# A hybrid decoder step on one core: the order of the q, k and v projections in the attention's input stage

## The chip, the core and the metric

The kernel runs on one core of a Trainium2 chip. Its time is the device time of one launch in microseconds (us), the median of several runs. The core has a matrix engine (TensorE; PE for its products, PEld for its weight loads), a vector engine (VectorE, DVE), a scalar engine (ScalarE, ACT), a third engine for elementwise work (GpSimd, POOL), and SyncE (SP), whose instruction stream issues most of the DMAs. Every engine works through its own list of instructions in order, and an instruction that waits holds back what is behind it on the same engine. The engines' working memory is SBUF, the products' results land in eight banks of PSUM, and inputs, outputs and scratch arrays lie in HBM.

## What is computed

One layer of a decoder. The input, 1024 prompt rows and 64 sample rows (1088 in all), is normalised and multiplied with one wide weight matrix `w_in`, whose columns belong to three groups of heads: a recurrent mixer (RWKV-7, here "wkv"), a short convolution, and a stick-breaking attention of 8 heads of 64. Their outputs go through an output projection, an MLP and a gated embedding.

```python
h = rmsnorm(x, g_mix)
proj = h @ w_in                                   # [wkv 1024 | convolution 768 | attention 3 x 512]
o_rw, wkv_new, shift_new = rwkv7_mixer(p_rw, ...)
cb, cc, cx = split(p_cv, 3); o_cv = short_conv_mixer(cb, cc, cx, ...)
q, k, v = [t.reshape(B, T, 8, 64) for t in split(p_sb, 3)]
q, k = rmsnorm(q, q_gain), rmsnorm(k, k_gain)     # over the 64 of each head; v is left as it is
o_sb = stick_breaking(q, k_all, v_all, past_len, sb_bias)
x = x + concat(o_rw, o_cv, o_sb) @ w_out
x = x + square(relu(rmsnorm(x, g_mlp) @ w_up)) @ w_down
x = x + sigmoid(rmsnorm(x, g_ple) @ w_ple_gate) * (p @ w_ple_proj)
```

The new k and v rows of all tokens are outputs too.

## The kernel before

All large products are made in three passes: an operand is kept as a high part (rounded to the fast 32-bit format `F32R`) and a low part (the rest), and hi*hi, lo*hi and hi*lo are added up in one bank.

The stages follow one another in the text: the input's norm and transposes; the wkv projections (`rw_tile`, lines 316 to 339, called in the loop of line 374); the wkv chunks (`wkv_prompt_chunks`, line 658, called in line 761); the attention's input stage (lines 767 to 865); then the wkv sample chunk, the convolution and the attention's first half (lines 1030 to 1032); the output projection and the rest. A scheduler makes each engine's list ahead of time by simulating the program: an instruction that stands earlier in the text goes first when it is ready in that simulation, and later ones fill the time between. So the products of the attention's input stage fill PE while the wkv work of the stage before is still going on, at places that the simulation chose and that no longer move when the program runs.

Of the wkv work two parts matter here. `wkv_base` (line 267), called in line 424, inverts small triangular blocks for all 16 chunks. It loads `base_Z` from scratch (SP, line 276), then alternates 31 times between a product (DVE, line 281, from 1 up to 961 elements per partition) and a sum (DVE, line 283), each waiting for the one before, copies the result (line 284) and stores it in `t_s` (SP, line 285). `wkv_local` (line 463) then loads a pair of chunks: `ar` and `bk` (SP, lines 483 and 486) and the inverse `TT` (line 491). Its first products are in line 508. The pool of these tiles (`kp`, line 760) is laid over the pool of `wkv_base`, which is released in line 759, so that the loads wait for the tiles that were there before.

The attention's input stage makes q (n = 0), k (n = 1) and v (n = 2) of two halves of the heads (hf = 0, 1, four heads or 256 columns each): six projections. Each has five steps (i0 = 0, 2, 4, 6, 8), of two tiles of 128 tokens, or one tile in the last step, which holds the sample rows.

- `W.load` (line 147) brings the 1024x256 weights in two pieces of 512 KB (SP, line 156), rounds them (ACT, line 158) and makes the low part (POOL, line 159). There are two buffers for each of raw piece, high and low part.
- `project` (line 782): per tile 24 products of 256 columns (PE, lines 791 to 793) into one of two banks in turn (`gemm_sb`), then a copy to a tile `nat` (ACT, line 798; five buffers). For q and k alone follow the square (ACT, line 801), the sum over each head (DVE, line 803), the root (ACT, line 804), the reciprocal (DVE, line 805) and the scaling of `nat` (DVE, line 806).
- `keep` (line 809): for k the gain is multiplied on POOL into `kg` (line 816). k and v rows go to the outputs (SP, lines 820 to 824). For v, except in the last step, each of the two tiles is split into a tile `spl`: high part on ACT (line 830), low part on DVE (line 831), a store to `v_s` on SP (line 832).
- `stack` (line 834), for q and k only and not for the last step: four transposes of `nat` on PE (line 840) into bank 2, the high part with the gain (ACT, line 842), the low part (DVE, line 843), and four stores to `stk_s`, two on ACT's and two on SP's list (line 846). `spl` and these two tiles share four buffers (tag `st`).

A stack isn't made right after its step: steps wait in a list `waiting`, and the oldest is taken out when two wait; `tc.issue_after(last.ins)` puts its transposes behind the last product of the current step in PE's list. When v comes, the list is emptied. The tiles of this stage are in a pool `sbp`, released in line 865; the convolution's pool `cv` (line 966) takes its place. The convolution uses the same two banks (line 967), the wkv sample chunk uses bank 2 (line 1030), and the attention's `prep` (line 878) loads heads 0 to 7 one after the other from `stk_s` and `v_s`.

Of the kernel before, what the change touches and what calls it, by code (L numbers as in the profile page):

```python
# [48 lines left out]
def hybrid_step(ctx: ExitStack, tc: tile.TileContext, I, O):  # L49
# [6 lines left out]
    def f(t):  # L56
        return t.bitcast(F32)
# [115 lines left out]
    w_in = I["w_in"][0]  # L173
    W = Weights(wpool)
# [139 lines left out]
    last = rp.tile([9, 1024], F32, name="last")  # L314
# [452 lines left out]
    SB0 = 1792  # L767
# [14 lines left out]
    def project(hf, n, w, i0):  # L782

        ni = min(2, 9 - i0)
        ps = gemm_sb()[:, :256 * ni]
        for i in range(ni):
            t0 = min(128 * (i0 + i), T - 128)
            o = ps[:, 256 * i:256 * i + 256]
            for k in range(8):
                a, b = (x[k // 4][:, k % 4, t0:t0 + 128] for x in hT)  # L790
                PE.matmul(o, a, w[0][:, k, :], start=(k == 0), stop=False)  # L791
                PE.matmul(o, a, w[1][:, k, :], start=False, stop=False)  # L792
                last = PE.matmul(o, b, w[0][:, k, :], start=False, stop=(k == 7))  # L793
        nat = sbp.tile([128, 2, 256], F32, name="nat", bufs=5)
        flat = nat.rearrange("p i c -> p (i c)")[:, :256 * ni]
        n4 = flat.rearrange("p (g d) -> p g d", d=64)
        m = 4 * ni
        S.copy(flat, ps)
        if n < 2:
            sq = sbp.tile([128, 512], F32, name="sq", bufs=1)  # L800
            S.square(sq[:, :256 * ni], ps)
            ss = sbp.tile([128, 8], F32, name="ss", bufs=3)
            V.reduce_sum(ss[:, :m], sq[:, :256 * ni].rearrange("p (g d) -> p g d", d=64), axis=AX.X)
            S.activation(ss[:, :m], ss[:, :m], AF.Sqrt, bias=eps_rms, scale=1.0 / 64)
            V.reciprocal(ss[:, :m], ss[:, :m])
            V.tensor_mul(n4, n4, ss[:, :m, None].to_broadcast([128, m, 64]))
        return nat, last

    def keep(hf, n, i0, nat):

        hs, cs = slice(4 * hf, 4 * hf + 4), slice(256 * hf, 256 * hf + 256)
        ni = min(2, 9 - i0)
        out = nat
        if n == 1 or n == 0 and i0 == 8:
            out = sbp.tile([128, 2, 256], F32, name="kg", bufs=2)
            G.tensor_mul(*(t.rearrange("p i c -> p (i c)")[:, :256 * ni].rearrange("p (g d) -> p g d", d=64)
                           for t in (out, nat)), gains[:, n, None, :].to_broadcast([128, 4 * ni, 64]))
        dst_p, dst_s = outs[n]
        if i0 == 8:
            SP.dma_start(new_s[n][:, cs], out[64:128, 0])  # L820
            if n:
                SP.dma_start(dst_s[0].rearrange("b j h d -> (b j) (h d)")[:, cs], out[64:128, 0])
        elif n:
            SP.dma_start(dst_p[0, 0].rearrange("t h d -> t (h d)")[i0 * 128:i0 * 128 + 256, cs]
                         .rearrange("(i p) c -> p i c", p=128), out)
        if n == 2 and i0 < 8:
            for i in range(2):
                src = nat[:, i].rearrange("p (h d) -> p h d", h=4)
                spl = sbp.tile([128, 4, 128], F32R, name="spl", tag="st", bufs=4)
                S.copy(spl[:, :, 0:64], src)  # L830
                V.tensor_sub(spl[:, :, 64:128], src, f(spl[:, :, 0:64]))
                SP.dma_start(v_s[hs, i0 + i].rearrange("h p e -> p h e"), f(spl))
# [16 lines left out]


    waiting = []
    for hf in range(2):
        for n in range(3):
            w = W.load(w_in[:, SB0 + 512 * n + 256 * hf:SB0 + 512 * n + 256 * hf + 256])
            for i0 in range(0, 9, 2):
                nat, last = project(hf, n, w, i0)
                keep(hf, n, i0, nat)
                while waiting and (len(waiting) > 1 or n == 2):
                    with tc.issue_after(last.ins):
                        stack(*waiting.pop(0))  # L860
                    if n < 2:
                        break
                if n < 2 and i0 < 8:
                    waiting.append((hf, n, i0, nat))
    sbp.release()


# [684 lines left out]
    for sl in range(4):  # L1552
        w = load(wg_[:, sl * 256:sl * 256 + 256], 8, 256)
# [35 lines left out]
```

## Time and profile before

| what | us |
|---|---|
| median of 3 runs (lowest and highest) | 1735.58 (1730.76 to 1736.79) |
| the profiled execution, its own time | 1743.91 |
| its span, first to last instruction | 1742.0 |
| PE busy in the span | 1663.5 (95%) |
| DVE busy | 1109.6 (64%) |
| ACT busy | 774.8 (44%) |
| POOL busy | 693.0 (40%) |
| mean granted TensorE clock | 0.978 of full speed |

The profile is of one execution. An engine is called busy while one of its instructions runs; the ends of PE's products are modelled and products overlap, so that PE's busy share alone doesn't tell how close it is to its peak: the distance from one product's start to the next does. "Idle before, releaser" is the time that an engine stood still and the instruction or DMA that ended the wait. Times within the span count from its first instruction. The attention's input stage runs from about 155 to 448 us.

### The profile page before, as it was taken

The numbers are of one execution on the slowest core, as the hardware profiler recorded it, in microseconds if no ns is written. First come the engines' busy times: TensorE is split into PE (matmuls) and PEld (weight loads), VectorE is DVE, ScalarE is ACT, GpSimd is POOL, SyncE is SP. The second block draws the span as 40 slices with busy tenths as digits, with TensorE's granted clock in tenths as the row PEclk, the third lists the DMA queues.
The fourth block names the chain that finished last, engine by engine and source line by source line (L and its number), as shares of the span: only waits on it lengthen the run. The fifth ranks groups of instructions, "written<-read, shape, count | busy, mean of one in ns | idle before, by whom it ended". The sixth has DMA issues, their size and how long they took to land.

```text
span 1742.0 us, 30723 instructions
## 1 busy us (share of the span) xinstructions
PE 1663.5 (95%) x11901; PEld 1496.9 (86%) x11901; DVE 1109.6 (64%) x1830; ACT 774.8 (44%) x1537; POOL 693.0 (40%) x746
## 2 busy tenths in 40 slices
PE   6999889999999889999999999998999999998998
PEld 5898888888998667888887767988899999998898
DVE  6266863554576659878754444467888878876432
ACT  6634323323353658566543433464444343443421
POOL 4133121212331654433434652376665555544210
PEclk9999999999999899999999999999999999998999
DMA  5134456434623753443244553421322232321211
GB/s 185 50 115 133 104 156 163 118 88 133 160 75 81 247 174 103 126 125 105 88 142 145 180 175 114 162 67 61 106 89 89 86 94 86 94 94 55 64 52 40
DMA packets 207059, 197.01 MB, mean 113 GB/s; under 512 B 58113, under 2 KB 172449, under 8 KB 206786
## 3 DMA queue, kind: packets, MB, share of 16 engines
q1 hardware_dynamic: 197186, 174.08, 33.5%
q0 software_dynamic: 5120, 16.78, 3.2%
q10 hardware_dynamic: 4608, 4.20, 1.0%
q8 instruction: 93, 1.52, 0.4%
q14 instruction: 52, 0.43, 0.1%
HBM read 158.02 MB, written 36.98 MB: 112 GB/s over the span
## 4 chain that ended last, share of the span: by engine, by line
PE 73%; DVE 12%; DMA 5%; issue 3%; ACT 2%; SPq 2%; POOL 1%; ACTq 0%; DVEq 0%; POOLq 0%
PE b L1087 13%; PE b L1089 13%; PE b L1088 13%; PE b L1416 3%; PE b L1415 3%; PE b L1414 3%; PE b L169 2%; PE b L170 2%; PE b L171 2%; DVE base_Q L281 2%; PE b L791 2%; PE b L792 2%; PE b L793 2%; PE b L936 1%; DMA wr<-in_w_out 1%
## 5 line engine op out<-in xcount | busy, mean ns | idle before, releaser
L1068 POOL TENSOR_TENSOR wl<-wr,wh 128x512 fp32r<-128x512 f32 x172 | 236.0, 1381 | 269.1 <-ACT wh L1067 260.2
L1067 ACT CAST wh<-wr 128x512 fp32r<-128x512 f32 x292 | 179.1, 621 | 305.2 <-PE b L1088 205.9
L1087 PE MATMUL b<-ah,wh 128*128 128x288 f32 (+1 forms) x768 | 258.9, 337 | 10.9 <-DVE x L1452 7.9
L1452 DVE TENSOR_TENSOR x<-b,x 128x288 f32<-128x288 f32 (+1 forms) x384 | 199.0, 528 | 98.4 <-PE b L1089 94.0
L1089 PE MATMUL b<-ah,wl 128*128 128x288 f32 (+1 forms) x768 | 254.8, 332 | 0.0
L1088 PE MATMUL b<-al,wh 128*128 128x288 f32 (+1 forms) x768 | 254.1, 331 | 0.0
L1087 PEld LDWEIGHTS b<-ah,wh 128*128 128x128 f32 x768 | 146.7, 191 | 25.7 <-DVE x L1452 12.5
L1087 PE MATMUL b<-nh,wh 128*128 128x512 f32 (+1 forms) x448 | 165.2, 370 | 0.1
L1088 PE MATMUL b<-nl,wh 128*128 128x512 f32 (+1 forms) x448 | 164.9, 368 | 0.3 <-DVE nl L1297 0.3
L1089 PE MATMUL b<-nh,wl 128*128 128x512 f32 (+1 forms) x448 | 164.2, 367 | 0.0
L1089 PEld LDWEIGHTS b<-ah,wl 128*128 128x128 f32 x768 | 146.7, 191 | 11.3 <-issue 0.8
L1088 PEld LDWEIGHTS b<-al,wh 128*128 128x128 f32 x768 | 147.0, 191 | 9.7 <-issue 0.8
L791 PE MATMUL b<-wh,h_hi 128*128 128x256 f32 x432 | 129.2, 299 | 0.0
L159 POOL TENSOR_TENSOR wl<-wr,wh 128x1024 fp32r<-128x1024 f32 x26 | 69.2, 2673 | 149.0 <-ACT wh L158 114.7
L792 PE MATMUL b<-wl,h_hi 128*128 128x256 f32 x432 | 127.0, 294 | 0.0
L793 PE MATMUL b<-wh,h_lo 128*128 128x256 f32 x432 | 125.9, 291 | 0.0
L169 PE MATMUL b<-h_hi,wh 128*128 128x384 f32 (+1 forms) x336 | 115.5, 344 | 1.9 <-ACT xs L330 1.2
L170 PE MATMUL b<-h_lo,wh 128*128 128x384 f32 (+1 forms) x336 | 113.2, 337 | 0.0
L171 PE MATMUL b<-h_hi,wl 128*128 128x384 f32 (+1 forms) x336 | 111.9, 333 | 0.0
L916 DVE TENSOR_TENSOR_SCAN keep<-keep,onesq 128x128 f32<-128x128 f32 (+3 forms) x64 | 94.7, 1481 | 20.9 <-POOL keep L914 19.7
L1068 DVE TENSOR_TENSOR wl<-wr,wh 128x512 fp32r<-128x512 f32 x120 | 100.6, 841 | 6.0 <-ACT wh L1067 3.1
L1068 POOL TENSOR_TENSOR wsl<-s,wsh 128x512 fp32r<-128x512 f32 x64 | 88.5, 1405 | 29.3 <-ACT wsh L1067 29.2
(417 smaller groups left out, 4326.3 us busy)
## 6 DMA issues: line engine op xcount, KB each, us to landing
wr<-in_w_up SPq DMA_DIRECT2D x64, 512.0 KB
wr<-in_w_down SPq DMA_DIRECT2D x64, 512.0 KB
wr<-in_w_in SPq DMA_DIRECT2D x26, 512.0 KB
wr<-in_w_out SPq DMA_DIRECT2D x16, 512.0 KB
xt<-in_x_prompt SPq DMA_DIRECT2D x8, 512.0 KB
stk_s<-sth ACTq DMA_DIRECT2D x32, 128.0 KB
stk_s<-stl SPq DMA_DIRECT2D x32, 128.0 KB
v_s<-spl SPq DMA_DIRECT2D x16, 256.0 KB
```

The source lines that it names most:

```text
L169: PE.matmul(ps[:, :n], wh[:, k, c], a, start=(k == 0), stop=False)
L170: PE.matmul(ps[:, :n], wh[:, k, c], b, start=False, stop=False)
L171: PE.matmul(ps[:, :n], wl[:, k, c], a, start=False, stop=(k == nk - 1))
L791: PE.matmul(o, a, w[0][:, k, :], start=(k == 0), stop=False)
L792: PE.matmul(o, a, w[1][:, k, :], start=False, stop=False)
L793: last = PE.matmul(o, b, w[0][:, k, :], start=False, stop=(k == 7))
L1067: S.copy(h3, src)
L1068: (sub or G).tensor_sub(l3, src, f(h3))
L1087: PE.matmul(ps[:, :n], w(0, k, m), a, start=(k == 0), stop=False)
L1088: PE.matmul(ps[:, :n], w(0, k, m), b, start=False, stop=False)
L1089: PE.matmul(ps[:, :n], w(1, k, m), a, start=False, stop=(k == nk - 1))
L1452: V.tensor_add(p.x[:, m, t0:t0 + n], ps[:, :n], p.x[:, m, t0:t0 + n])
```

## The change

The six projections come in another order. Before, each half of the heads has q, k, v: (hf, n) = (0,0), (0,1), (0,2), (1,0), (1,1), (1,2). After, v of both halves is first, then q and k of the first half, then q and k of the second: (n, hf) = (2,0), (2,1), (0,0), (1,0), (0,1), (1,1). The list of waiting stacks is treated alike in all steps (the oldest is taken when two wait), and what is left is stacked behind the last product of all. No instruction is added or taken away.

```diff
     waiting = []
-    for hf in range(2):
-        for n in range(3):
-            w = W.load(w_in[:, SB0 + 512 * n + 256 * hf:SB0 + 512 * n + 256 * hf + 256])
-            for i0 in range(0, 9, 2):
-                nat, last = project(hf, n, w, i0)
-                keep(hf, n, i0, nat)
-                while waiting and (len(waiting) > 1 or n == 2):
-                    with tc.issue_after(last.ins):
-                        stack(*waiting.pop(0))
-                    if n < 2:
-                        break
-                if n < 2 and i0 < 8:
-                    waiting.append((hf, n, i0, nat))
+    for n, hf in ((2, 0), (2, 1), (0, 0), (1, 0), (0, 1), (1, 1)):
+        w = W.load(w_in[:, SB0 + 512 * n + 256 * hf:SB0 + 512 * n + 256 * hf + 256])
+        for i0 in range(0, 9, 2):
+            nat, last = project(hf, n, w, i0)
+            keep(hf, n, i0, nat)
+            if len(waiting) > 1:
+                with tc.issue_after(last.ins):
+                    stack(*waiting.pop(0))
+            if n < 2 and i0 < 8:
+                waiting.append((hf, n, i0, nat))
+    for args in waiting:
+        with tc.issue_after(last.ins):
+            stack(*args)
     sbp.release()
```

## The prediction

> **What bounds the kernel now.** I read the chain that ended last, then busy time by stretches, PE's waits, and DVE's groups where the chain lies on DVE.
>
> ```profile
> PE 73%; DVE 12%; DMA 5%; issue 3%; ACT 2%; SPq 2%; POOL 1%; ACTq 0%; DVEq 0%; POOLq 0%
> ```
>
> PE carries the chain, DVE the next largest part. The stretches (PE, PEld, DVE, ACT and POOL busy with their counts, clock, DMA share, GB/s) say where PE isn't full:
>
> ```profile
> 155.00:256.00 101.00, 85.02 (x706) 83.04 (x705) 79.89 (x122) 28.96 (x55) 28.47 (x15) 0.93 0.53 143
> 256.00:290.00 34.00, 32.53 (x320) 29.56 (x318) 9.89 (x23) 7.16 (x16) 2.92 (x2) 0.90 0.68 175
> 290.00:448.00 158.00, 158.00 (x1916) 139.19 (x1916) 83.81 (x186) 53.43 (x120) 35.60 (x40) 1.00 0.44 114
> 448.00:557.00 109.00, 108.43 (x819) 98.31 (x818) 74.22 (x151) 50.03 (x110) 33.67 (x80) 0.98 0.40 107
> ```
>
> From 290 to 557 us PE is full at full clock: there only less PE work would help, and the change takes none away. From 155 to 256 us PE idles 16 of 101 us at a mean clock of 0.93. All waits of PE from 155 to 448 us (total, times, longest):
>
> ```profile
> PE b L840 <- DVE stl L843: 9.4, 3, 4.8
> PE b L442 <- DVE LT L262: 3.3, 1, 3.3
> PE b L840 <- DVE nat L806: 3.1, 1, 3.1
> PE b L621 <- ACT UV L564: 1.3, 1, 1.3
> ```
>
> So 9.4 + 3.1 = 12.5 us are the stacks' transposes, which wait for DVE. DVE is late since it runs the wkv base inversion then. Its first and last instruction, with DVE's groups between them:
>
> ```profile
> 177.62 0.16 DVE L281 TENSOR_TENSOR base_Q<-base_Z,base_X 128x1 f32<-128x1 f32 x1 [6.21 <-DMA base_Z<-l_s]
> 238.66 2.03 DVE L284 COPY base_X<-base_X 128x1024 f32<-128x1024 f32 x1
> ```
> ```profile
> L281 DVE TENSOR_TENSOR base_Q<-base_Z,base_X 128x1 f32<-128x1 f32 (+30 forms) x31 | 26.9, 867 | 6.8 <-DMA base_Z<-l_s 6.2
> L283 DVE TENSOR_REDUCE base_X<-base_Q 128x1 f32<-128x1 f32 (+30 forms) x31 | 15.5, 500 | 0.5
> L806 DVE TENSOR_TENSOR nat<-nat,ss 128x512 f32<-128x512 f32 (+1 forms) x10 | 11.4, 1140 | 0.0
> L803 DVE TENSOR_REDUCE ss<-sq 128x8 f32<-128x512 f32 (+1 forms) x10 | 6.2, 624 | 0.0
> L843 DVE SCALAR_TENSOR_TENSOR stl<-b,gainT,sth 128x512 fp32r<-128x512 f32 x6 | 4.5, 745 | 0.0
> L284 DVE COPY base_X<-base_X 128x1024 f32<-128x1024 f32 x1 | 2.0, 2028 | 0.0
> L805 DVE RECIPROCAL ss<-ss 128x8 f32<-128x8 f32 (+1 forms) x10 | 1.9, 188 | 0.0
> ```
>
> The inversion alone is 26.9 + 15.5 + 2.0 = 44.4 us and lasts 63.1 us (177.6 to 240.7), since 11.4 + 6.2 + 4.5 + 1.9 = 24.0 us of q's and k's work sit between its steps (sums overlap a little). The way from its end to the first wkv product goes through SP's list:
>
> ```profile
> 240.72 0.34 SPq L285 DMA_DIRECT2D t_s<-base_X  x1
> 242.79 1.24 SPq L846 DMA_DIRECT2D stk_s<-stl  x2
> 247.15 2.05 SPq L483 DMA_DIRECT2D ar<-ar_s  x2
> 251.85 0.98 SPq L486 DMA_DIRECT2D bk<-bk_s  x2
> ```
> ```profile
> 256.35 0.71 PE L508 MATMUL b<-ar,bk 64*128 64x128 f32 x8
> ```
>
> The loads are issued to 252.8 us; the product starts at 256.35 with no wait before it. PE had lost so much to the transposes that it got there about when the data did: the two losses are one loss seen twice, and that decides how much the change can give.
>
> **What the change does, and what each part costs.**
>
> 1. *Transposes out of the inversion's time.* With v first, nothing that PE does for two projections waits for DVE: a bank is freed by ACT's copy alone. The 12.5 us of waits go from their place. With them goes the slow clock behind each:
>
> ```profile
> 183.70 0.65 PE L840 MATMUL b<-ident,nat 128*128 128x128 f32 x4 [3.11 <-DVE nat L806]
> 186.21 0.41 PE L792 MATMUL b<-wl,h_hi 128*128 128x256 f32 x1
> 186.42 0.41 PE L793 MATMUL b<-wh,h_lo 128*128 128x256 f32 x1
> 188.31 0.28 PE L792 MATMUL b<-wl,h_hi 128*128 128x256 f32 x1
> 188.43 0.28 PE L793 MATMUL b<-wh,h_lo 128*128 128x256 f32 x1
> ```
>
> After the wait of 3.11 us starts are 0.21 us apart, and two us later 0.12. I estimate 1.6 us lost behind a wait (some 3.6 us of products at this pace), 4.8 us for the three long ones. PE would reach its place at 256.35 us up to 12.5 + 4.8 = 17.3 us sooner. That is the most that this part gives; the least is nothing, if PE then waits as long for the wkv data.
>
> [...]
>
> 2. *The inversion gets DVE sooner.* v's work on DVE is one subtraction per tile:
>
> ```profile
> L831 DVE TENSOR_TENSOR spl<-nat,spl 128x256 fp32r<-128x256 f32 x16 | 7.0, 468 | 12.6 <-ACT spl L830 12.6
> ```
>
> All 16 take 7.0 us. PE needs 48 x 0.12 = 5.8 us for a full step and 432 x 0.12 = 52 us for both of v's projections, so by about 155 + 52 + 3.3 (the wait for LT, which stays) + 2 for wkv's own products, 212 us, v is projected, and two steps of q come before the inversion ends; without their stacks that is 2 x (0.62 + 0.19 + 0.68 by the normal length of L806, an estimate from 11.4 us less the two long ones) = 3 us. The inversion would end at 177.6 + 44.4 + 7.0 + 3.0 = 232 us, 8.7 us sooner. From both sides: if none of q's steps and none of POOL's interference falls in it, 12 us sooner; if each subtraction in DVE's list waits for ACT as the 12.6 us in its row did, 4 us sooner or nothing. POOL's interference:
>
> ```profile
> 198.02 2.85 DVE L806 TENSOR_TENSOR nat<-nat,ss 128x512 f32<-128x512 f32 x1
> 201.13 2.85 DVE L281 TENSOR_TENSOR base_Q<-base_Z,base_X 128x441 f32<-128x441 f32 x1
> 204.66 1.06 DVE L281 TENSOR_TENSOR base_Q<-base_Z,base_X 128x484 f32<-128x484 f32 x1
> ```
> ```profile
> 197.92 5.22 POOL L159 TENSOR_TENSOR wl<-wr,wh 128x1024 fp32r<-128x1024 f32 x2 [34.15 <-PE b L840]
> ```
>
> While POOL makes weights' low parts, a product of 441 elements takes 2.85 us, where a larger one right after takes 1.06. The next weights are made in the inversion's time in either order, so I leave this in the 44.4.
>
> [...]
>
> 3. *What PE waits for instead.* The first wkv product can't come before the inversion's end and the 15.6 us behind it (240.7 to 256.35; stores of v take the place of the stacks' there): 232 + 15.6 = 247.6 us, or 244 with the 12 us. PE is there at 256.35 - 17.3 = 239 us, if the simulation puts as many projection products ahead of it as now. So PE waits 5 to 9 us (I take 7) once, and pays the clock once, 1.6 us. Behind that product in PE's list stand q's next steps, which are held back with it.
>
> 4. *The tail.* The stage now ends with k and its last stack, no longer with v.
>
> ```profile
> 447.20 0.28 PE L793 MATMUL b<-wh,h_lo 128*128 128x256 f32 x1
> 447.32 0.34 PE L169 MATMUL b<-h_hi,wh 128*128 128x384 f32 x1
> ```
> ```profile
> 451.73 0.48 ACT L981 COPY cc<-b 128x384 f32<-128x384 f32 x1 [1.94 <-PE b L171]
> ```
>
> The convolution follows without a gap, and its first copy, into memory that this pool leaves, waits only for its product. k's chain after the product is copy and square on ACT, 1.5 us on DVE (as above), and the gain on POOL:
>
> ```profile
> L816 POOL TENSOR_TENSOR kg<-nat,gains 128x512 f32<-128x512 f32 (+1 forms) x12 | 14.9, 1240 | 66.1 <-DVE nat L806 29.8 <-issue 12.5 <-ACT Yg L646 12.2
> ```
>
> With 1.2 us for that and an estimated 1.3 for ACT it is some 4 us, about what the convolution's first group takes (447.3 to 451.7), and two banks cover a second group: I take 1 us, between 0 and the 4 us of that chain. SP's stores for it stand ahead of the sample chunk's loads; PE being full from 448 to 557 us hides that.
>
> 5. *v's queues, which move into the inversion's time.*
>
> ```profile
> v_s<-spl SPq DMA_DIRECT2D x16, 256.0 KB
> ```
> ```profile
> ACT spl L830 <- DMA v_s<-spl: 3.6, 3, 2.8
> ```
>
> A step of v stores two such tiles and 256 KB of output, some 130 GB/s, where the first stretch shows a DMA share of 0.53: hidden. SP's stores wait for the subtraction, at most one product of the inversion late (1 to 2.9 us), and the next weights' loads stand behind them; these have a projection's 26 us. ACT's rounding waits for a buffer, and the copies that free PE's banks stand behind it. Before, that cost ACT 3.6 us and PE nothing; with four buffers, two steps' time, I take nothing. Without that cover PE would wait those 3.6 us.
>
> Sum: 17.3 - 7 - 1.6 - 1 = 7.7, about 8 us. The profiled execution took 1743.9 us (span 1742.0, 1.9 outside); it would take 1735.9. It lies 8.3 above the median of the runs shown, so the forecast is 1735.6 - 8 = 1727.6 us.
>
> **The rivals.**
>
> *All of it.* The simulation finds the wkv data later relative to the projections than the chip does, or puts more projection products ahead of them; PE never waits for L508, and only the tail is paid: 17.3 less 1 = 16 us, 1719.5. For it: the list is made anew, and four full projections are left to fill with. Against: the lists now fell out so that data and PE met at 256 us only because PE was late.
>
> *Nothing.* The inversion is no earlier (its subtractions wait for ACT, POOL stretches them), PE stands still the whole 17 us at L508 instead of at the transposes: 1735.6 within 3. For it: DVE is 80 of 101 us busy; against: 24 us of DVE work become 10.
>
> *Slower: DVE becomes late in the wkv chunks.* From 256 to 447 us DVE has now ten q or k steps:
>
> ```profile
> L803 DVE TENSOR_REDUCE ss<-sq 128x8 f32<-128x512 f32 (+1 forms) x10 | 6.3, 629 | 9.6 <-ACT sq L801 9.6
> ```
>
> After, some 18 of the 20 fall there. Each of the eight more puts up to 0.68 + 0.75 = 1.4 us (L806, L843) in front of a DVE step of the wkv chain, and PE's list is fixed. If all hit it, PE waits 11 us, and with four of these waits long enough for the slow clock, 6 more: 17 - 8 = 9 us slower, 1744.6. It decides from 8 us of such waits on. Against it: with ten steps PE waited not once from 290 to 448 us, and DVE's share there is 84 of 158, 100 of 158 after.
>
> **The numbers.** Forecast (4 to 13 us faster, 1722.6 to 1731.6) 0.46; all of it 0.18; nothing 0.18; slower 0.18. A measurement tells about 0.5%, 8.7 us, from no change. Half of the forecast's chance, 0.24, and all of the first rival's is faster by more: 0.42. The other 0.22 and "nothing" are within: 0.40. Slower 0.18. The range goes from the first rival less the runs' own 3 us and a bit, 1715, to the slower case, 1745.
>
> **What would show it.** The row L840 <- L806 or L843 is gone from PE's waits before 240 us, and the inversion's copy (L284) ends near 232 us, not 240.7. PE has one new wait, before L508, of 5 to 9 us, which ends near 247. ACT no longer waits for L803 until v is done. From 290 us on PE has no waits, and the convolution's first product follows the last projection within 1 us, at about 439. I am wrong if L284 ends after 238 us, if PE's new wait is over 12 us or absent, or if waits for DVE appear among the wkv chunks.

## The result, and the profile after

The changed kernel took 1747.33 us (median of 6 runs, 1742.29 to 1748.82), the kernel before 1735.82 us beside it (6 runs, 1730.76 to 1738.13): ratio 1.0063 with a 95% interval of 1.0044 to 1.0083. It is 11.5 us slower, outside the predicted range of 1715 to 1745 us.

Most of what the prediction named as a sign came. PE's waits in the changed kernel from 150 us to its last projection (total, times, longest) are two:

```profile
PE b L508 <- DMA bk<-bk_s: 11.3, 1, 11.3
PE b L442 <- DVE LT L262: 3.5, 1, 3.5
```

The 12.5 us of L840 are gone and the one new wait stands before L508, but it is longer than the 5 to 9 us forecast. There is no wait for DVE among the wkv chunks. The timelines of the changed kernel show where the new wait comes from (start, length, engine, instruction); DVE's, SP's and PE's:

```profile
228.37 1.16 DVE L284 COPY base_X<-base_X 128x1024 f32<-128x1024 f32 x1
```
```profile
229.55 0.33 SPq L285 DMA_DIRECT2D t_s<-base_X  x1
229.98 0.46 SPq L820 DMA_DIRECT2D new<-nat  x1
230.49 1.43 SPq L822 DMA_DIRECT2D out<-nat  x1
232.02 1.16 SPq L156 DMA_DIRECT2D wr<-in_w_in  x1
233.27 1.04 SPq L483 DMA_DIRECT2D ar<-ar_s  x2
...
237.07 0.87 SPq L486 DMA_DIRECT2D bk<-bk_s  x2
```
```profile
227.57 0.28 PE L793 MATMUL b<-wh,h_lo 128*128 128x256 f32 x1
239.17 1.23 PE L508 MATMUL b<-ar,bk 64*128 64x128 f32 x8 [11.33 <-DMA bk<-bk_s]
```

The inversion ends at 229.5 us, the data are there 9.6 us later, and PE stands still from 227.8 us on. The prediction had put the data at 247.6 us, 15.6 us behind the inversion, and PE at 239 us: both came sooner, PE by more. Behind the wait the granted clock was 0.50 until 247.0 us, 7.9 us long, with products 0.21 us apart instead of 0.12; that is some 3.4 us lost (an estimate from these figures). PE comes so early because less work stands ahead of L508 in its list. The groups of PE's instructions up to that product, kernel before and changed kernel (busy, mean ns, idle before):

```profile
L791 PE MATMUL b<-wh,h_hi 128*128 128x256 f32 x200 | 59.6, 298 | 0.0
L792 PE MATMUL b<-wl,h_hi 128*128 128x256 f32 x199 | 58.3, 293 | 0.0
L793 PE MATMUL b<-wh,h_lo 128*128 128x256 f32 x199 | 58.0, 292 | 0.0
L840 PE MATMUL b<-ident,nat 128*128 128x128 f32 x32 | 5.9, 316 | 12.5 <-DVE stl L843 9.4 <-DVE nat L806 3.1
```
```profile
L791 PE MATMUL b<-wh,h_hi 128*128 128x256 f32 x179 | 52.2, 292 | 0.0
L793 PE MATMUL b<-wh,h_lo 128*128 128x256 f32 x179 | 51.2, 286 | 0.0
L792 PE MATMUL b<-wl,h_hi 128*128 128x256 f32 x179 | 51.0, 285 | 0.0
```

598 projection products and 32 transposes became 537 products and none. The new list has 61 products (7.3 us at 0.12 us from start to start) behind L508 that stood ahead of it; that the scheduler's simulation had the inversion end earlier too is the likely reason, and isn't shown. PE is at L508 28.5 us sooner (227.8 against 256.35): 12.5 us are the waits, 7.3 these products, and the other 8.7 the 32 transposes and the slow clock behind the waits, which weren't told apart.

The two profiled executions differ by only 2.7 us (1743.91 and 1746.60), since the one before lay 8 us above its median. So the comparison is made with a second pair, profiled side by side on one other chip (the runs before_third and after_third below, ratio 1.0080), cut at the last projection's last product (here at its end, in the table further down at its start), the output projection's first product (L1087), the attention's last (L946) and the first product of the gated embedding's stage (L1414). First the kernel before (us, then busy time and count of PE, PEld, DVE, ACT, POOL, the granted clock, DMA share, GB/s); its second row is the first 17 us behind the last projection:

```profile
150.00:441.30 291.30, 276.75 (x2954) 252.18 (x2953) 174.25 (x335) 89.52 (x191) 66.79 (x57) 0.97 0.51 134
441.30:458.30 17.00, 17.00 (x104) 17.00 (x103) 10.37 (x32) 4.14 (x7) 5.73 (x6) 1.00 0.73 196
458.30:585.00 126.70, 117.36 (x912) 103.52 (x911) 87.95 (x165) 69.26 (x157) 44.02 (x106) 0.95 0.44 130
585.00:890.00 305.00, 298.36 (x1520) 250.50 (x1519) 230.40 (x296) 184.03 (x357) 129.59 (x168) 0.98 0.40 121
890.00:1188.60 298.60, 289.75 (x1864) 235.49 (x1863) 142.98 (x219) 130.31 (x244) 147.94 (x138) 0.99 0.44 136
1188.60:1733.00 544.40, 523.97 (x3727) 508.26 (x3725) 375.70 (x674) 214.11 (x434) 250.63 (x199) 0.99 0.26 81
```

The changed kernel:

```profile
150.00:438.80 288.80, 271.50 (x2947) 248.72 (x2946) 172.49 (x334) 88.46 (x187) 63.24 (x56) 0.96 0.50 131
438.80:455.80 17.00, 10.09 (x59) 9.45 (x59) 14.53 (x34) 5.04 (x9) 6.71 (x4) 0.87 0.69 183
455.80:593.00 137.20, 125.81 (x964) 112.00 (x964) 87.97 (x160) 68.68 (x156) 43.78 (x107) 0.95 0.43 130
593.00:902.80 309.80, 300.31 (x1531) 251.55 (x1530) 243.45 (x303) 184.62 (x363) 139.61 (x170) 0.99 0.40 120
902.80:1201.20 298.40, 289.44 (x1853) 234.98 (x1852) 138.06 (x218) 128.23 (x241) 146.50 (x137) 0.98 0.44 136
1201.20:1746.00 544.80, 526.30 (x3727) 509.93 (x3725) 378.47 (x674) 215.08 (x434) 249.96 (x199) 0.99 0.26 81
```

That is the account of the 13.0 us between these two spans (1732.9 and 1745.9): the last projection 2.5 us sooner; from it to L1087 154.2 instead of 143.7 us, 10.5 more; the attention's second half 4.8 more; nothing behind it (-0.2 and +0.4). The front's gain is small because the idle time stayed: PE idles 17.3 us from 150 us to the last projection, 14.6 before the change. And in the first 17 us behind it PE runs 59 instructions where it ran 104. Of the 10.5 us 9.0 are idle time of PE (18.3 against 9.3 us); the rest is busy time, in which the eight transposes of the last two stacks, which now stand behind the last projection, have a part.

The three longest waits of that stretch, kernel before and then the changed one:

```profile
PE b L946 <- DVE o L950: 4.5, 2, 3.5
PE b L936 <- DVE wtl L61: 1.5, 1, 1.5
PE b L907 <- ACT keep L910: 1.1, 1, 1.1
```
```profile
PE b L907 <- DMA stk_q<-stk_s: 6.2, 1, 6.2
PE b L946 <- DVE o L950: 4.5, 3, 2.7
PE b L936 <- DVE beta L918: 3.2, 1, 3.2
```

What PE stands behind is seen in the first profile of the changed kernel: SP's timeline, then DVE's and POOL's.

```profile
442.22 0.47 SPq L873 DMA_DIRECT2D bias<-in_sb_bias  x1
447.14 1.23 SPq L846 DMA_DIRECT2D stk_s<-stl  x2
448.42 0.59 SPq L888 DMA_DIRECT2D stk_k<-stk_s  x1
...
450.26 0.79 SPq L888 DMA_DIRECT2D stk_q<-stk_s  x1
```
```profile
440.68 1.93 DVE L281 TENSOR_TENSOR base_Q<-base_Z,base_X 16x25 f32<-16x25 f32 x1
...
442.84 2.14 DVE L281 TENSOR_TENSOR base_Q<-base_Z,base_X 16x36 f32<-16x36 f32 x1
...
445.23 0.24 DVE L281 TENSOR_TENSOR base_Q<-base_Z,base_X 16x49 f32<-16x49 f32 x1
...
446.39 0.73 DVE L843 SCALAR_TENSOR_TENSOR stl<-b,gainT,sth 128x512 fp32r<-128x512 f32 x1
```
```profile
440.16 4.75 POOL L159 TENSOR_TENSOR wl<-wr,wh 128x1024 fp32r<-128x1024 f32 x2
```

SP issues nothing from 442.7 to 447.1 us: at the head of its list stands the store of a low part of k (L846), which DVE makes only at 446.39 us, though its high part was through on ACT at 441.95: DVE goes through the sample chunk's small inversion first, whose products are stretched while POOL makes the convolution's weights (16x25 elements take 1.93 us and 16x36 2.14, against 0.24 for 16x49 right behind). Behind that store stand the loads of the attention's first head, and PE stands at their first product (L907). In the kernel before, v's steps were the last, and the same inversion ran (452 to 463 us in the first profile) under products of the convolution, of which 120 stand ahead of the attention's first.

### The profile page after: what moved, and what is told of

Its sections match the earlier page's. It is cut to its first block, busy times and chain, and to the rows that moved or that the text cites. A ratio compares the mean times of both kernels' runs of the same rounds, so it can differ in the third digit from the quotient of the medians.

```text
span 1744.9 us, 30708 instructions
## 1 busy us (share of the span) xinstructions
PE 1655.5 (95%) x11901; PEld 1490.2 (85%) x11901; DVE 1114.0 (64%) x1830; ACT 773.1 (44%) x1537; POOL 701.8 (40%) x746
## 4 chain that ended last, share of the span: by engine, by line
PE 77%; DVE 10%; DMA 4%; issue 3%; ACT 2%; POOL 1%; SPq 1%; another core or an unknown queue 0%; ACTq 0%; DVEq 0%; POOLq 0%
PE b L1087 13%; PE b L1088 13%; PE b L1089 13%; PE b L1416 3%; PE b L1415 3%; PE b L1414 3%; PE b L793 3%; PE b L791 3%; PE b L792 3%; PE b L169 2%; PE b L170 2%; PE b L171 2%; PE b L936 2%; PE b L508 1%; DVE base_Q L281 1%
## 5 line engine op out<-in xcount | busy, mean ns | idle before, releaser
L1068 POOL TENSOR_TENSOR wl<-wr,wh 128x512 fp32r<-128x512 f32 x172 | 245.3, 1434 | 300.4 <-ACT wh L1067 246.3
L1087 PE MATMUL b<-ah,wh 128*128 128x288 f32 (+1 forms) x768 | 258.4, 337 | 14.9 <-DVE x L1452 12.3
L1089 PE MATMUL b<-ah,wl 128*128 128x288 f32 (+1 forms) x768 | 253.9, 331 | 0.0
L1087 PEld LDWEIGHTS b<-ah,wh 128*128 128x128 f32 x768 | 145.8, 190 | 32.2 <-DVE x L1452 18.4
L1087 PE MATMUL b<-nh,wh 128*128 128x512 f32 (+1 forms) x448 | 164.3, 368 | 2.5 <-DVE x L1375 2.5
L1089 PE MATMUL b<-nh,wl 128*128 128x512 f32 (+1 forms) x448 | 163.5, 365 | 0.0
L1089 PEld LDWEIGHTS b<-ah,wl 128*128 128x128 f32 x768 | 146.1, 190 | 11.0
```

The source lines that it names most:

```text
L1068: (sub or G).tensor_sub(l3, src, f(h3))
L1087: PE.matmul(ps[:, :n], w(0, k, m), a, start=(k == 0), stop=False)
L1089: PE.matmul(ps[:, :n], w(1, k, m), a, start=False, stop=(k == nk - 1))
```

## The experiments

The first theory, "the tail": k at the stage's end costs what the front gained. Its rival, "the lists": moving v makes every later list anew, and the loss lies there. The five groups of kernels below ran on a chip each, the kernel before beside them. This table gives for each the start of the last projection's last product, and the time from there to L1087, to the attention's last product, to L1414 and to the end (us, from the traces' first and last starts of these lines):

| run | last projection | to L1087 | to L946's last | to L1414 | to the end |
|---|---|---|---|---|---|
| before_again | 445.8 | 142.4 | 304.6 | 286.1 | 543.7 |
| tail_only | 445.5 | 152.6 | 306.0 | 285.0 | 544.9 |
| one_v_first | 435.2 | 147.9 | 311.1 | 285.2 | 549.2 |
| act_stores | 437.7 | 155.4 | 307.9 | 286.7 | 544.7 |
| att_later | 435.6 | 148.0 | 323.6 | 311.8 | 544.6 |
| b_att_later | 452.7 | 139.7 | 320.1 | 312.0 | 544.9 |
| rule_only | 443.6 | 140.9 | 303.8 | 300.1 | 547.7 |
| no_last_stacks | 434.3 | 151.6 | 308.8 | 299.4 | 547.5 |
| after_again | 435.6 | 155.9 | 309.2 | 309.2 | 544.7 |
| flush_soon | 440.7 | 151.9 | 310.5 | 306.8 | 549.4 |
| q_last | 437.1 | 153.3 | 309.1 | 310.6 | 544.8 |
| one_v_rule | 436.5 | 148.0 | 307.1 | 311.3 | 544.6 |
| before_third | 441.1 | 144.0 | 305.0 | 298.5 | 544.4 |
| after_third | 438.5 | 154.5 | 309.8 | 298.4 | 544.7 |
| base_early | 457.1 | 150.7 | 307.3 | 296.3 | 546.2 |
| b_base_early | 448.1 | 148.2 | 300.1 | 295.1 | 545.0 |
| rule_again | 444.8 | 138.4 | 303.2 | 286.5 | 542.2 |
| q_v_k | 445.1 | 142.6 | 308.9 | 284.0 | 544.6 |

### The same kernel again (before_again)

> The kernel before once more, unchanged. Its first profiled execution took 1743.9 us, 8 us above the median of its runs (1735.8), while that of the changed kernel (1746.6) lay at its median (1747.3); so a comparison of those two traces shows only 2.7 of the 11.5 us. Either theory expects a median within 3 us of 1735.8, and a profiled execution near it shows which stretch the 8 us came from. It also gives the ratio that two equal kernels show here: 1.000 within 0.0015.

1.0003 (0.9984 to 1.0022). This span is 19.4 us shorter than that of the first profile (1722.6 and 1742.0), and only 2.9 us of it lie ahead of the attention's end: the stage with the gathers behind it takes 286.1 us, not 297.1, and the rest 543.7, not 549.3. So profiles of different chips are compared here up to the attention's end, not behind it.

### k at the end, front as before (tail_only)

```diff
-    for n, hf in ((2, 0), (2, 1), (0, 0), (1, 0), (0, 1), (1, 1)):
+    for n, hf in ((0, 0), (1, 0), (2, 0), (2, 1), (0, 1), (1, 1)):
```

> The order is q, k of the first half, v of both halves, then q and k of the second half: the inversion meets q and k as in the kernel before, and the stage ends as in the changed kernel. Theory 'the tail' (k's last steps and stacks meet the sample chunk's inversion on DVE and stand in SP's list ahead of the loads of the attention's first head): the transposes still wait some 9 to 13 us for DVE before 240 us, PE again stands 4 to 8 us at the attention's first product (L907), and the kernel is 6 to 16 us slower than before, 1742 to 1752 us. Rival 'the lists' (the loss comes in later stages, whose lists are made anew, from v being early): no wait of over 2 us at L907, and the time is within 4 us of before, 1732 to 1740.

1.0048 (1.0032 to 1.0065). The last projection comes as before (445.5 against 445.8), and from there to L1087 it takes 10.2 us more. This kernel has the changed rule for the waiting stacks too; against rule_only and rule_again further down, which have that rule as well and differ from it only in the place of v's second half, the stretch is 11.7 and 14.2 us longer (other chips). So the order of the end alone makes the tail's loss. The place was not the expected one, and the transposes ahead of 240 us waited 6.8 us for DVE where 9 to 13 were expected. PE's three longest waits in the stretch:

```profile
PE b L708 <- DMA s_in<-in_state_wkv: 4.2, 2, 3.9
PE b L936 <- DVE beta L918: 4.1, 2, 3.8
PE b L169 <- ACT cc L981: 2.7, 1, 2.7
```

L907 waits 1.1 us only. The loss is the stage's, the place depends on the list.

### v of the first half first, of the second half last (one_v_first)

```diff
-    for n, hf in ((2, 0), (2, 1), (0, 0), (1, 0), (0, 1), (1, 1)):
+    for n, hf in ((2, 0), (0, 0), (1, 0), (0, 1), (1, 1), (2, 1)):
...
-            if len(waiting) > 1:
+            while waiting and (len(waiting) > 1 or n == 2):
...
+                if n < 2:
+                    break
```

> v of the first half comes first, v of the second half last, q and k of both halves between: part of the changed kernel's front and the kernel before's end. Theory 'the tail': the transposes' waits before 240 us are under 4 us in all, no wait over 2 us at the attention's first product (L907), the convolution's products follow the last projection without a gap, and the kernel is 4 to 9 us faster than before, 1727 to 1732 us. Rival 'the lists': it is as slow as the changed kernel or between, 1740 to 1748, without a wait at L907.

1.0008 (0.9991 to 1.0025): no gain, against the first theory, and the transposes' waits fell to 6.1 us only, where under 4 were expected. It reaches the last projection 10.6 us sooner than before_again, gives back 5.5 us by L1087, with v at the end and no wait of over 1.2 us at the attention's first product (L907 before), and 6.5 more in the attention's second half. So the rival has a part: some loss comes with a new list.

### k's last stores from ACT (act_stores)

```diff
-                (S, SP)[e].dma_start(stk_s[...]
+                (S, S if (hf, n) == (1, 1) else SP)[e].dma_start(stk_s[...]
```

> The changed kernel with one edit: the low parts of the last projection's stacks (k of the second half) are stored from ACT's list, no longer from SP's, so that nothing of k stands in SP's list ahead of the attention's loads. Theory 'the tail', with SP's list as the carrier: PE's wait at L907 (6.4 us in the changed kernel) falls under 2 us, its slow clock after 454 us goes too, and the time falls by 5 to 9 us, from 1747 to 1738 to 1742. If DVE's lateness is the carrier (the sums and low parts of k between the steps of the sample chunk's inversion) and not SP's list, L907 still waits 4 us or more and the time stays within 3 us of 1747. Rival 'the lists': the wait goes and the time stays at 1747 too.

1.0060 (1.0039 to 1.0080), as the changed kernel. PE's four longest waits behind the last projection:

```profile
PE b L936 <- DVE beta L918: 5.0, 3, 3.4
PE b L907 <- ACT keep L910: 3.1, 1, 3.1
PE b L946 <- DVE o L950: 2.1, 2, 1.2
PE b L840 <- DVE stl L843: 2.0, 1, 2.0
```

The wait for the loads is gone, the stretch is as long (155.4 us). PE comes to L907 5.4 us sooner (449.2 against 454.6) and now waits for DVE and ACT. SP's list was the last to end; it alone doesn't decide.

### The attention later in the text (att_later, b_att_later)

```diff
+    for _ in range(6):
+        next(conv)
     run(*[conv] * CA[0], *[att] * CA[1])
```

> The changed kernel, and the convolution's first six groups of products stand ahead of the attention in the text, so that the attention's first products come later in PE's list. In the changed kernel PE stands 10 us more than before between the last projection and the first product of the output projection, at the attention's first products and transposes (L907 6.4 us, L936 3.5, L946 and L947 6.3). Theory 'started too soon' (the loads and k's last work on DVE aren't through when the attention begins, and that is all): the wait at L907 goes, PE's idle time in that stretch falls from 18 to 8 to 10 us, and the kernel is 6 to 12 us faster than the changed one, 0 to 4 us faster than the kernel before. Rival 'the same DVE work, later': the waits move to L936, L946 or to the sample chunk, the stretch stays within 4 us, and the time is 0.4 to 0.8% above the kernel before, as the changed kernel.

> The same six groups put ahead of the attention in the kernel before: what this edit does by itself. In the kernel before PE has no wait of over 1.2 us between 447 and 477 us, so there is nothing for it to remove: within 4 us of the kernel before by either theory; if it is over 4 us faster, a gain of att_later is not the cure of the tail but of this stage as such.

1.0136 (1.0113 to 1.0160) on the changed kernel, 1.0070 (1.0049 to 1.0091) on the kernel before: both expectations missed. The edit itself costs some 15 us in the attention's second half (323.6 and 320.1 us; that it has less of the convolution left to fill with is the likely reason, not shown), and in att_later L907 still waits 6.3 us. The stretch to L1087 shrank to 148.0 us, but more than that was lost behind it, so the pair says nothing on the cure.

### The waiting stacks' rule alone (rule_only, rule_again)

```diff
-    for n, hf in ((2, 0), (2, 1), (0, 0), (1, 0), (0, 1), (1, 1)):
+    for n, hf in ((0, 0), (1, 0), (2, 0), (0, 1), (1, 1), (2, 1)):
```

> The order of the kernel before, but the waiting stacks are treated as in the changed kernel: the oldest is taken when two wait, in v's steps too, and what is left is stacked at the end. Of each half's ten stacks the last then comes during the next projection's first steps instead of in v's first two steps. Theory 'the tail': the last stack of k waits through v's steps no longer than in the kernel before and the end of the stage has v's work alone, so the time is within 3 us of before. Rival 'the lists' (any new list costs): 4 us or more slower.

> The order of the kernel before with the changed kernel's rule for the waiting stacks, once more on another chip. If its gain is its list's, 0.996 to 0.999 of the kernel before; if it was a chance of that chip, 0.999 to 1.002.

0.9974 (0.9958 to 0.9990) and 0.9982 (0.9963 to 1.0002): the half of the diff that isn't the order gains 3 to 4.5 us, where rule_only was expected within 3 us of before or slower. In their traces the way from the last projection to L1087 is shorter (140.9 and 138.4 us, against 142.4 and 144.0 in two of the kernel before). It is the only version here that beat the kernel before, on one chip clearly; the other chip's interval reaches 1.0002.

### Without k's last two stacks (no_last_stacks)

```diff
+                if (hf, n, i0) in ((0, 1, 0), (0, 1, 2)):
+                    (S, SP)[e].dma_start(stk_s[1, 4 + s:8:2, e, :, 1024 + i0 * 128 - 512:1024 + i0 * 128 - 256]
+                                         ...
...
-            if len(waiting) > 1:
+            if len(waiting) > 1 and (hf, n, i0) != (1, 1, 8):
...
-    for args in waiting:
-        with tc.issue_after(last.ins):
-            stack(*args)
```

> The changed kernel without the last two stacks of k's second half (steps i0 = 4 and 6: eight transposes, two roundings, two low parts, eight stores): that part of k's stacked copy is left out, and in its place rows of an earlier stack are stored there, ahead of time. Theory 'k's stacks carry the tail' (their low parts and stores are what the attention's first head stands behind): PE's wait at L907 falls under 2 us and the time falls by 6 to 10 us against the changed kernel, to within 0.2% of the kernel before. If k's other work on DVE (the sums and scalings of its last steps between those of the sample chunk's inversion), or the attention's early place as such, is the carrier, the time falls by the 2 us of the eight transposes and their clock at most and stays 0.4% or more above the kernel before.

1.0019 (0.9999 to 1.0039), where the changed kernel had 1.0063 to 1.0118. The attention's first products (L907 before) wait 0.4 us for their loads, and 2.7 for ACT. The stretch to L1087 is 151.6 us: with the stacks gone it is shorter by some 3 to 4 us, not by 10. They carry a part, in which the eight transposes themselves are counted; an earlier last projection (434.3 us) is the rest of the gain up to the attention's end.

### The changed kernel again, stacks sooner, and q at the end (after_again, flush_soon, q_last)

> The changed kernel once more, unchanged, on the chip of the next three. What the stages behind the attention take differs between executions of kernels that are alike there (the gather stage took 124.9 to 148.6 us in the runs so far), so the stages are compared by the end of the attention: 902.9 us in the first profile of the changed kernel, 895.7 and 892.8 in two of the kernel before. Every theory expects 1.0044 to 1.0083 of the kernel before, and the attention's end again at 900 to 905 us.

```diff
-            if len(waiting) > 1:
+            while len(waiting) > (hf + n < 2 or i0 < 4):
```

> The changed kernel, and in the last projection the stacks follow one step after their own step, so that one stack is left for the end and not two; every stack is still made. Theory 'k's stacks carry half of the tail' (without two of them the kernel was 0.44% nearer to the kernel before): the last low part (L843) and its stores come 3 to 6 us earlier, the waits at L907 together fall by 3 us or more, and the time falls by 2 to 5 us against the changed kernel, to 1.001 to 1.005 of the kernel before. Rival (what counts is that any stack or sum of k falls into the sample chunk's inversion): within 2 us of the changed kernel.

```diff
-    for n, hf in ((2, 0), (2, 1), (0, 0), (1, 0), (0, 1), (1, 1)):
+    for n, hf in ((2, 0), (2, 1), (0, 0), (1, 0), (1, 1), (0, 1)):
```

> The order of the changed kernel with k of the second half ahead of q of the second half: the stage ends with q, whose last projection has the same sums, scalings and stacks on DVE, but no gain on POOL and, but for the sample rows, no stores to the outputs. If the stacks and sums on DVE carry the tail: within 3 us of the changed kernel, 1.005 to 1.008 of the kernel before. If k's gain on POOL and its output stores in SP's list carry it: 4 us or more faster than the changed kernel, 1.000 to 1.004.

after_again 1.0118 (1.0089 to 1.0147), above what was expected; the attention ends at 900.7 us, as expected. On that chip the gather stage takes 309.2 us, 298.4 in after_third. flush_soon 1.0114 (1.0085 to 1.0143): L907's wait falls from 6.3 to 4.3 us and the stretch by 4 us, but the last projection comes 5.1 us later and the time is after_again's, as the rival expected. q_last 1.0082 (1.0054 to 1.0110): its median is 2.4 us below after_again's and the intervals overlap; k's gain and its output stores aren't the main cost, a small part stays open.

### Both edits joined (one_v_rule)

```diff
-    for n, hf in ((2, 0), (2, 1), (0, 0), (1, 0), (0, 1), (1, 1)):
+    for n, hf in ((2, 0), (0, 0), (1, 0), (0, 1), (1, 1), (2, 1)):
```

> v of the first half first, v of the second half last, and the waiting stacks treated as in the changed kernel. The two edits that this joins gave 1.0008 (v of the first half first, v of the second last) and 0.9974 (the rule alone). If the gains of the front and of the rule add up, and the end is that of the kernel before: 0.994 to 0.998 of the kernel before. If each new list costs a few us by itself, which is the rival that one_v_first spoke for: 0.998 to 1.004.

1.0038 (1.0017 to 1.0059), in the rival's range: the gains don't add up. The lead of some 10 us at the last projection is partly gone by L1087 again (148.0 us).

### Both kernels side by side, and the small inversion moved (before_third, after_third, base_early, b_base_early)

> The kernel before, unchanged, for a profile on the same chip as the next three. Ratio 1.000 within 0.002. The attention ends at 892 to 897 us, and from there to the first product of the gated embedding's stage (L1414) it takes 286 us on a chip where the gathers are quick and about 300 us where they are slow.

> The changed kernel, unchanged, on the same chip. The attention ends at 900 to 905 us, 7 to 10 us behind the kernel before. Theory 'the gathers cost it more': from there to L1414 it takes 5 us or more longer than the kernel before where the gathers are slow, and the whole is 1.008 or more; where they are quick both take the same within 2 us and the whole is 1.004 to 1.008. Rival: the stage costs both the same on any chip, and all of the loss is there at the attention's end.

0.9993 (0.9976 to 1.0010) and 1.0080 (1.0059 to 1.0101). The stages behind the attention take the same (298.5 and 298.4, 544.4 and 544.7 us): here the loss is complete at the attention's end. It comes at 890.1 and 902.8 us, 12.7 us apart where 7 to 10 were expected.

```diff
     def wkv_sample_chunk(bank):
         sp = kp
-        wkv_base(kp, 1, 16, l_s[1], t_s[1], ("um", "GS", "um"), (2, 1, 2))
...
+    wkv_base(kp, 1, 16, l_s[1], t_s[1], ("Yg", "UV", "Yg"), (2, 3, 2))
     wkv_prompt_chunks()
```

> The changed kernel with the sample chunk's inversion (15 pairs of product and sum on DVE, some 12 us with the gaps) ahead of the wkv prompt chunks instead of at the start of the sample chunk, so that none of it falls together with k's last steps, and on DVE it can follow the large inversion while PE waits for the first chunk's loads. Theory 'k's last steps meet the inversion': the stretch from the last projection to the output projection's first product shrinks from 156 us to under 148, the waits at L907 under 3 us, and the kernel is 6 to 12 us faster than the changed one, at most 1.002 of the kernel before, unless DVE's extra 12 us at 230 us hold up the chunks. Rival (the tail is lost to the attention and its fixed lists, with or without the inversion): within 4 us of the changed kernel.

> The kernel before with the sample chunk's inversion ahead of the wkv prompt chunks. There the inversion (451 to 463 us) ends before the attention's first product (467.5) and lies under 120 products of the convolution, so the tail has nothing to gain: either theory expects the time within 4 us of the kernel before, or slower, as DVE has 12 us more to do around 240 us, when PE waits for it. If it is faster by 4 us or more, a gain of base_early is one of this stage as such and no cure of the changed order.

base_early 1.0104 (1.0067 to 1.0141), b_base_early 1.0001 (0.9984 to 1.0019). With the small inversion out of the tail the stretch falls from 154.5 to 150.7 us and L907 waits 2.5 us (for ACT), but the front pays: its last projection comes at 457.1 us, behind this wait of PE:

```profile
PE b L508 <- DVE base_Q L281: 13.4, 1, 13.4
```

So the inversion too is a part of the tail, some 4 us, and no place was free of charge. Between the two kernels with this edit the stretch differs by 2.5 us (150.7 and 148.2), where it differs by 10.5 without it; but 4.2 of these 8 us are there because the kernel before became slower in that stretch. From one profile of each it can't be said whether the meeting of k and the inversion is the cause or the new lists are.

### v between q and k of the first half (q_v_k)

```diff
-    for n, hf in ((2, 0), (2, 1), (0, 0), (1, 0), (0, 1), (1, 1)):
+    for n, hf in ((0, 0), (2, 0), (1, 0), (0, 1), (1, 1), (2, 1)):
```

> The rule alone, and in the first half of the heads v comes between q and k: q, v, k, then q, k, v of the second half. Fewer stacks fall into the large inversion, and the end of the stage is as before. If the front's gain can be had without the tail's loss: the transposes' waits before 240 us fall under 6 us, no wait of over 2 us at L907, and the time is 0.993 to 0.998 of the kernel before. If what PE wins before L508 is lost there or in later lists: 0.998 to 1.004, as the two kernels with v of the first half first (1.0008 and 1.0038).

1.0025 (1.0007 to 1.0042), as the rival expected. The tail is as before (142.6 us). PE's waits up to 445 us show the front by itself:

```profile
PE b L508 <- DMA bk<-bk_s: 12.3, 1, 12.3
PE b L442 <- DVE LT L262: 3.5, 1, 3.5
PE b L840 <- DVE nat L806: 1.3, 1, 1.3
PE b L840 <- DVE stl L843: 0.5, 1, 0.5
```

In rule_again, the same kernel without this edit on the same chip, the transposes wait 7.6 us and L508 2.9. So 5.8 us of the first are gone, and 9.4 more stand at L508; the last projection comes at 445.1 us, in rule_again at 444.8. The wait was moved, not removed.

## Why the prediction was wrong

Set against the prediction's own sum, in the pair from one chip: the front gave 2.5 us, not 17.3 - 7 - 1.6 = 8.7; the tail cost 10.5, not 1; and the attention's second half, which stood in no term, cost 4.8. That is 20.5 us less than the 7.7 forecast, 12.8 us slower, and the two spans differ by 13.0.

1. *Transposes out of the inversion's time*: right. 12.5 us of waits (10.5 in before_third) became none.
2. *The inversion gets DVE sooner*: right. It ends at 229.5 us where 232 was forecast, and in the pair from one chip at 231.0 instead of 238.5 us. v's subtractions took 8.9 us in all, 7.0 before the change.
3. *What PE waits for instead*: mechanism right, size wrong. 7 us were taken, 5 to 9 given; it measured 11.3, and 13.8 in after_third. The step rested on "if the simulation puts as many projection products ahead of it as now". It put 61 fewer there, and the 32 transposes, whose own time the 17.3 us left out, weren't ahead of it either; so PE was at L508 at 227.8 us, not 239, and the inversion's lead went into standing still. The way from the inversion's end to that product was 9.6 us, not 15.6: the 15.6 were read where PE, not the data, came last. And the slow clock behind the wait, put at 1.6 us, cost some 3.4. The prediction had called the two waits "one loss seen twice" and yet booked 17.3 us of one against 7 of the other. In q_v_k, against rule_again, they cancel. What was left is 2.5 us in the pair from one chip and 9.5 in the first two profiles.
4. *The tail*: the step that failed. It was put at 1 us, 4 at most, and "PE being full from 448 to 557 us hides that" covered SP's stores. It measured 10.5 us in the pair from one chip, and 10.2 in tail_only, where the front is as before (11.7 and 14.2 against the two runs with the same rule for the stacks). PE was full there because v was the end: five steps with nothing for DVE but v's subtractions, so that k's sums, scalings and stacks were through (the last low part began at 421.3 us) when the small inversion began at 452 us. In the changed kernel the inversion begins at 436.5 us, among k's last steps, and the last low part at 451.3. The cover was a property of the order that the change takes away, and the working looked only at k's own chain. No single carrier was found: SP's stores, the two last stacks, their place and the inversion were each taken out alone, and at most some 4 us of the stretch came back each time; where the wait for the loads was gone, PE met the next late thing on DVE or ACT. So the loss is shown to hang on the order of the end, and how it splits among these stays open.
5. *v's queues*: right. ACT waited 10.5 us for v's stores (3.6 before), but no wait of PE stands on them.

Not in the working at all: 4.8 us in the attention's second half, 2.9 of them idle time of PE. Eleven instructions more fall into it (1531 against 1520; ten are products of L1087 to L1089), which the stretch behind has fewer (1853 against 1864) without being shorter. It doesn't hang on k at the end: q_v_k, with the old end, takes 308.9 us there too, one_v_first 311.1. Which feature of the new lists does it was not found.

Of the rivals, *all of it* fell with the 11.3 us, *nothing* was nearest for the front, and *slower* had the sign with the wrong place: DVE became late, but not in the wkv chunks (PE has no wait from 290 to 437 us in after_third); it became late at the stage's end. The forecast's own signs (L284 early, one new wait, none among the chunks) held in the first profile but for the wait's size and end (11.3 us and 239.2, not 5 to 9 and 247); in after_third, at 13.8 us, it passes the 12 that the prediction had named as a sign of being wrong. They were signs of the front, and there was none for a late tail but the convolution's first product.

## What to carry to other kernels

Work that is light for the second engine is a cover that something uses wherever it stands; before moving it forward, ask what it covered at the place that it leaves, and read that stretch with the cover taken off. Where lists are fixed ahead of time, a wait removed ahead of data that are late anyway comes back at the data: count the products that stand ahead of the waiting one, and don't take their number as given. And a lead at the end of one stage is worth only what the next stage, with its own list, can start early.

## What the runs showed of the hardware that was not expected

The small inversion's products in the tail went from 16x25 elements in 1.93 us and 16x36 in 2.14 us, while POOL made weights' low parts, to 16x49 in 0.24 us right behind: an eighth of the time for more elements, where 441 elements on 128 rows had been stretched 2.7 times (2.85 to 1.06 us, with 484). Both long products end within 0.1 us of the POOL subtraction during which they began: at 442.61 and 444.98 us, where POOL's two pieces end at 442.55 and 444.91. The kernel before has one such product as well, 16x4 elements in 2.20 us up to 454.61, beside a subtraction from 452.19 to 454.59. Over the whole small inversion it is less, 15 products in the changed kernel (after_third) and before (before_third):

```profile
L281 DVE TENSOR_TENSOR base_Q<-base_Z,base_X 16x1 f32<-16x1 f32 (+14 forms) x15 | 9.0, 602 | 0.3
```
```profile
L281 DVE TENSOR_TENSOR base_Q<-base_Z,base_X 16x1 f32<-16x1 f32 (+14 forms) x15 | 6.5, 434 | 5.3 <-DMA base_Z<-l_s 4.9
```

The clock fell well before the wait at L508 was over: PE's last product ahead of it ends at 227.85 us, and the granted clock was 1.00 up to 230.0 us, 2.1 us behind that product, and 0.50 from there to 247.0. In the kernel before it was 1.00 all through the wait of 3.34 us at L442 and behind it (162 to 170.5 us); in the changed kernel the same wait, of 3.51 us, had 0.50 behind it (165.6 to 167 us).

The stage from the attention's end to L1414 took 284 to 312 us by chip and list. On one chip rule_only and no_last_stacks took 300, att_later and b_att_later 312; on another, the kernel before, the changed kernel and the two with the inversion moved took 295 to 299. In after_again PE waits 7.7 us at its products with gathered rows, in before_again not at all:

```profile
PE b L1231 <- issue: 7.7, 14, 1.0
```

What these waits end on is not in the profile, and whether this stage makes the changed kernel's ratio differ between chips (1.0063, 1.0080, 1.0118) was not shown.
